# First stage of a transformer block: products begun on unnormalised tokens, norm factors put in behind the product

## The chip, the core and the metric

The kernel runs on one core of a Trainium2 chip. The core has TensorE (PE: matmuls; PEld is its weight load), VectorE (DVE), ScalarE (ACT), GpSimd (POOL) and SyncE (SP, which here only issues DMAs). Each engine works through its own queue of instructions in order; a matmul writes a bank of PSUM, from where VectorE or ScalarE read it. The metric is the device time of one execution in microseconds; lower is better. Three runs of the kernel before gave 1831.18, 1831.6 and 1834.9 us.

## The reference

One layer in fp32 for 1024 tokens of width 1024: a half-weighted SwiGLU feed-forward (inner width 2816), a mixer (short convolution and gated delta rule), another half-weighted feed-forward, and a last norm. The change touches the first feed-forward's input side alone:

```python
def rmsnorm(x, w, eps=NORM_EPS):
    xf = x.astype(jnp.float32)
    y = xf * lax.rsqrt(jnp.mean(xf * xf, axis=-1, keepdims=True) + eps)
    return (y * w.astype(jnp.float32)).astype(x.dtype)

def swiglu_ffn(x, w_in, w_out):
    gate, up = jnp.split(x @ w_in, 2, axis=-1)
    return (jax.nn.silu(gate) * up) @ w_out

h = h + 0.5 * swiglu_ffn(rmsnorm(h, ffn1_norm[layer]), ffn1_w_in[layer], ffn1_w_out[layer])
```

The norm's factor is one number per token, the gain one number per column of x. So the factor of a token can be put in on either side of the product with `w_in`.

## The kernel before

**Numbers.** Each fp32 operand is split into a rounded high part and the rest (`split`, L104 on ScalarE for the high part, L105 on VectorE for the low part), and a product is three matmuls: hi by hi (L197), lo by hi (L198), hi by lo (L199), function `mm3`. Tiles are 128 x 512; x lies transposed, so that a column of a tile is a token and a row one of 1024 inputs: 8 tiles for the first 512 tokens (`h[0]`), 8 for the others (`h[1]`).

**Pairs.** The gate and up weights are worked through in 22 pairs of 128 columns. A pair is a 2 x 2 block product by a Strassen-like scheme with seven products instead of eight, each of 4 quarters of the sum times 3 matmuls = 12 matmuls. In words of the code: the *first product* (A11 x B11, `run_p1`), whose bank is copied to SBUF (`copy_p1`, L387, ScalarE); the *second product* (A12 x B21, `run_p2`), summed onto the first in the same bank, which gives block C11, read by ScalarE's silu (L510); the two products of sums S1 x T1 and nS2 x T2; p7 (S3 x T3), p4 (A22 x T4) and p3 (S4 x B22). The first and second products are a pair's *heads*: they need only the first tokens, no sums. S1, S2, S3, S4 are sums of token tiles (`Blocks.sums`, L331/L332 and what follows), T1 to T4 sums of weight tiles (L112 on POOL, for the first two pairs L117 on VectorE), and all are split before use.

**Order.** Tasks with a load, a preparation and a run are issued in a written order; the loads go ahead on SP's queue, the preparations some tasks ahead of the runs, and sums, norm and stores hang on a count of the matmuls (`later`). A scheduler then orders what is not pinned (`keep_in_program_order`). In the first stage, the heads of five pairs (EARLY) come first, then the first two pairs' S1 T1 and nS2 T2 together, quarter by quarter (`both`), then the heads of the sixth pair; p7 of the first two pairs and the heads of the seventh follow (INSIDE = 2). From the third pair on, a pair's heads lie inside the pair ahead of it.

**The start.** The eight tiles of the first tokens are loaded first; ScalarE squares each (L240), VectorE adds the squares up (L242), four matmuls by ones give the column sums (L248), VectorE and POOL make the factor (L223, L225), and four transposes spread it over the partitions into a PSUM bank (L271). Meanwhile TensorE does 34 + 6 + 5 matmuls of zeros (L708), whose result nobody reads. Then each tile is multiplied by gain and factor (`norm1`, L307) and split, and the first product of four pairs is done quarter by quarter. The factor of the other 512 tokens comes from token rows (`xtok`; `row_square`, `by_rows`), is spread by L271 too, and goes in with the sums; `begin2` (L317, L318) prepares those tiles.

## Time and profile before

| what | us |
|---|---|
| median of three runs | 1831.6 |
| the profiled execution's own time | 1828.37 |
| its span | 1826.6 |
| TensorE busy | 1791.3 |
| VectorE, ScalarE, POOL busy | 1309.4, 737.2, 680.6 |

The page adds up one execution: busy time and count of each engine, the span in slices, the chain that ended last, and groups of instructions. A matmul's row in a timeline gives start and length; matmuls overlap, so the distance between starts is what one costs. The mean granted TensorE clock over the span was 0.994 of full speed.

### The profile page before, as it was taken

To read this page: it belongs to the slowest core of one execution; us is meant where nothing else is said; L and a number is where in the kernel's file an instruction comes from. 1 tells how busy PE (TensorE), PEld (TensorE's weight loads), DVE (VectorE), ACT (ScalarE), POOL (GpSimd) and SP (SyncE) were. 2 spreads that over 40 slices of the span, in tenths; PEclk is the share of its full clock that TensorE was granted. 3 is DMA by queue.
4 is the path that set the end of the run, shared out by engine and by line. 5 is a ranking of instruction groups with operands and counts; after the bars stand their busy time and mean duration, and the time that the engine had idled before them with its cause. 6 is when DMAs were issued, how large, how long until landed. Compare 5 with 4: busy or idle time off the path is not lost.

```text
span 1826.6 us, 24897 instructions
## 1 busy us (share of the span) xinstructions
PE 1791.3 (98%) x8508; PEld 1463.7 (80%) x8509; DVE 1309.4 (72%) x2040; ACT 737.2 (40%) x1478; POOL 680.6 (37%) x478
## 2 busy tenths in 40 slices
PE   9999999999999999999989999999999999999997
PEld 6788888888888887777778887788888888888886
DVE  8966666567766888977857566888656666677675
ACT  7423232323534554476342343552223222254443
POOL 0365554446342402234421113006544554435252
PEclk9999999999999999999989999999999999999998
DMA  7253443337974543488754485523443343488642
GB/s 260 70 172 116 146 137 126 134 116 226 317 265 144 170 141 123 131 253 268 232 160 147 133 277 179 188 76 115 151 144 115 137 146 126 170 292 281 203 142 89
DMA packets 194320, 311.41 MB, mean 170 GB/s; under 512 B 28176, under 2 KB 48656, under 8 KB 194192
## 3 DMA queue, kind: packets, MB, share of 16 engines
q1 hardware_dynamic: 191168, 304.51, 50.1%
q10 hardware_dynamic: 3024, 5.30, 0.9%
q8 instruction: 67, 1.10, 0.2%
q14 instruction: 61, 0.50, 0.1%
HBM read 226.87 MB, written 82.86 MB: 170 GB/s over the span
## 4 chain that ended last, share of the span: by engine, by line
PE 85%; DVE 6%; DMA 3%; issue 2%; ACT 2%; POOL 1%; SPq 0%; ACTq 0%; POOLq 0%; DVEq 0%
PE ps_ps L197 24%; PE ps_ps L199 24%; PE ps_ps L198 24%; PE ps_mm L197 3%; PE ps_mm L198 2%; PE ps_mm L199 2%; DVE cv L884 1%; PE ps_aux L982 1%; DVE wlo L105 1%; DVE sv L1135 1%; DVE xb L1139 1%; DMA raw<-w_in 1%; DMA h<-xT 1%; PE ps_aux L1008 0%; PE ps_ps L799 0%
## 5 line engine op out<-in xcount | busy, mean ns | idle before, releaser
L197 PE MATMUL ps_ps<-hi,whi 128*128 128x512 f32 x1400 | 545.8, 391 | 3.7 <-DVE h L1469 1.5
L198 PE MATMUL ps_ps<-lo,whi 128*128 128x512 f32 x1400 | 545.1, 389 | 0.1
L199 PE MATMUL ps_ps<-hi,wlo 128*128 128x512 f32 x1400 | 544.7, 390 | 0.1
L105 DVE TENSOR_TENSOR wlo<-T,whi 128x512 fp32r<-128x512 f32 x244 | 225.8, 939 | 131.6 <-ACT whi L104 130.9
L112 POOL TENSOR_TENSOR T<-raw 128x512 f32<-128x512 f32 x132 | 206.9, 1568 | 299.7 <-DVE wlo L105 112.8
L197 PEld LDWEIGHTS ps_ps<-hi,whi 128*128 128x128 f32 x1400 | 262.7, 188 | 63.4 <-ACT p L387 2.6
L105 DVE TENSOR_TENSOR wlo<-raw,whi 128x512 fp32r<-128x512 f32 x280 | 247.2, 893 | 90.5 <-ACT whi L104 86.9
L199 PEld LDWEIGHTS ps_ps<-hi,wlo 128*128 128x128 f32 x1400 | 262.8, 188 | 56.2 <-DVE wlo L105 1.5
L198 PEld LDWEIGHTS ps_ps<-lo,whi 128*128 128x128 f32 x1400 | 262.9, 188 | 54.7 <-DVE lo L105 0.8
L197 PE MATMUL ps_ps<-ghi,whi 128*128 128x512 f32 x616 | 241.3, 392 | 0.0
L199 PE MATMUL ps_ps<-ghi,wlo 128*128 128x512 f32 x616 | 240.9, 391 | 0.4 <-DVE wlo L105 0.4
L198 PE MATMUL ps_ps<-glo,whi 128*128 128x512 f32 x616 | 240.6, 391 | 0.0
L104 ACT CAST whi<-raw 128x512 fp32r<-128x512 f32 x280 | 169.1, 618 | 58.5 <-DMA raw<-w_in 21.8
L104 ACT CAST whi<-T 128x512 fp32r<-128x512 f32 x244 | 146.3, 616 | 75.7 <-POOL T L112 34.3
L105 DVE TENSOR_TENSOR glo<-raw,ghi 128x512 fp32r<-128x512 f32 x154 | 129.0, 838 | 51.4 <-ACT ghi L104 51.3
L197 PE MATMUL ps_mm<-hi,whi 128*128 128x512 f32 x384 | 158.0, 411 | 1.2 <-DVE u L452 1.2
L198 PE MATMUL ps_mm<-lo,whi 128*128 128x512 f32 x384 | 151.9, 396 | 0.0
L199 PE MATMUL ps_mm<-hi,wlo 128*128 128x512 f32 x384 | 151.6, 395 | 0.0
L199 PEld LDWEIGHTS ps_ps<-ghi,wlo 128*128 128x128 f32 x616 | 115.8, 188 | 26.5 <-DVE wlo L105 1.0
L198 PEld LDWEIGHTS ps_ps<-glo,whi 128*128 128x128 f32 x616 | 116.1, 188 | 25.6
L197 PEld LDWEIGHTS ps_ps<-ghi,whi 128*128 128x128 f32 x616 | 115.7, 188 | 25.2
L387 ACT COPY p<-ps_ps 128x512 f32<-128x512 f32 x50 | 29.0, 585 | 240.4 <-PE ps_ps L199 239.4
(238 smaller groups left out, 2259.8 us busy)
## 6 DMA issues: line engine op xcount, KB each, us to landing
raw<-w_in SPq DMA_DIRECT2D x264, 256.0 KB, 4.5
raw<-w_out SPq DMA_DIRECT2D x154, 256.0 KB, 4.4
raw<-w_qkv SPq DMA_DIRECT2D x36, 256.0 KB, 3.1
f1S<-S SPq DMA_DIRECT2D x33, 256.0 KB, 4.9
raw<-f1A SPq DMA_DIRECT2D x33, 256.0 KB, 4.1
raw<-f1S SPq DMA_DIRECT2D x33, 256.0 KB, 3.7
f2S<-S SPq DMA_DIRECT2D x33, 256.0 KB, 4.9
raw<-f2A SPq DMA_DIRECT2D x33, 256.0 KB, 4.5
```

Source lines behind the costliest of these rows:

```text
L104: tc.keep_in_program_order(nc.scalar.copy(out=hi, in_=src))
L105: nc.vector.tensor_tensor(out=lo, in0=src, in1=hi.bitcast(F32), op=ALU.subtract)
L112: tc.keep_in_program_order(nc.gpsimd.tensor_tensor(out=out, in0=in0, in1=in1, op=op))
L197: nc.tensor.matmul(out=ps, lhsT=whi, rhs=xhi, start=start, stop=False, skip_group_check=True)
L198: nc.tensor.matmul(out=ps, lhsT=whi, rhs=xlo, start=False, stop=False, skip_group_check=True)
L199: nc.tensor.matmul(out=ps, lhsT=wlo, rhs=xhi, start=False, stop=stop, skip_group_check=True)
L387: ins = nc.scalar.copy(out=self.p1[:, 3:HALF + 3], in_=self.x_ps)
L884: nc.vector.scalar_tensor_tensor(out=acc, in0=u[:, i:i + HALF], scalar=vcol(wc + i), in1=acc, op0=ALU.mult, op1=ALU.add)
L982: nc.tensor.matmul(out=ps[:, sl], lhsT=lhs[:, sl], rhs=rhs[:, sl], start=start, stop=stop)
L1135: nc.vector.tensor_tensor(out=tv, in0=lrow[:, lo:hi].unsqueeze(2).broadcast_to([nb, n, j + 1]), in1=xrow[:, 0:j + 1].unsqueeze(1).broadcas ...
L1139: nc.vector.tensor_tensor(out=xv, in0=xv, in1=tv, op=ALU.subtract)
```

## The change

The first tokens are split as they land, with their gain but without the norm's factor. The first product of four pairs begins on them while the squares are still being summed. The column sums stand ahead of the last quarter of those products, the spread of the factor behind it. ScalarE copies the factor from PSUM to SBUF (`rb0`, which shares a buffer with a tile of a later stage), and it goes in when a bank is read: the first product's bank is read by VectorE with a multiply (new L388) in place of ScalarE's copy, and C11 by VectorE with a multiply (new L510), which is followed by the silu on ScalarE in SBUF (new L512). This holds for all 22 pairs. The tiles themselves are multiplied by the factor later, for the sums S2, S3 and S4. The squares of token rows, that multiply and `begin2` are spread over the tasks of the heads. There are 12 matmuls of zeros instead of 45. The first four weight tiles are loaded between the first and the second token tile, the token rows later. The heads of six pairs stand ahead of the sums instead of five, and of one pair instead of two inside.

```diff
+        def landed(self, d):
+            sq = slot(F32, "sq")
+            tc.keep_in_program_order(nc.scalar.activation(out=sq, in_=self.hh[d], func=AF.Square))
+            if d:
+                nc.vector.tensor_tensor(out=self.acc, in0=self.acc, in1=sq, op=ALU.add)
+            else:
+                self.acc = sq
...
         def copy_p1(self):
             self.p1 = temp4(F32, "p1")
-            ins = nc.scalar.copy(out=self.p1[:, 3:HALF + 3], in_=self.x_ps)
-            if self.pinned:
-                tc.keep_in_program_order(ins)
+            if self.rb is None:
+                nc.scalar.copy(out=self.p1[:, 3:HALF + 3], in_=self.x_ps)
+            else:
+                nc.vector.tensor_tensor(out=self.p1[:, 3:HALF + 3], in0=self.x_ps, in1=self.rb, op=ALU.mult)
...
         def first(ps):
             c = temp4(F32, "c11")
+            if rb is not None:
+                nc.vector.tensor_tensor(out=c[:, 3:HALF + 3], in0=ps, in1=rb, op=ALU.mult)
+                ps = c[:, 3:HALF + 3]
             nc.scalar.activation(out=c[:, 3:HALF + 3], in_=ps, func=AF.Silu)
...
+        def split_raw(d):
+            src, gain = h[0][d], x.gain(d)
+            hi, lo = slot(F32R, "hi"), slot(F32R, "lo")
+            tc.keep_in_program_order(nc.scalar.activation(out=hi, in_=src, func=AF.Copy, scale=gain))
+            nc.vector.scalar_tensor_tensor(out=lo, in0=src, scalar=gain, in1=hi.bitcast(F32),
+                                           op0=ALU.mult, op1=ALU.subtract)
+            x.b["A11" if d < KH else "A12"][d % KH] = hi, lo
...
-            get_x(0, *range(KT))
-            tc.keep_in_program_order(nc.sync.dma_start(out=cs, in_=cst))
+            get_x(0, 0)
             for p in four:
                 p.get("B11")
+            get_x(0, *range(1, KT))
+            tc.keep_in_program_order(nc.sync.dma_start(out=cs, in_=cst))
...
-            norms[0].as_they_land(idle)
-            norms[0].spread()
-            idle(5)
+            for _ in range(12):
+                tc.keep_in_program_order(
+                    nc.tensor.matmul(out=idle_ps, lhsT=zero[:, 0:P], rhs=zero, start=True, stop=True))
             for p in four:
                 p.x_ps = psum()
-                p.ready("B11")
+            for k in range(KH):
+                split_raw(k)
+                if k == 0:
+                    for p in four:
+                        p.ready("B11")
+                norms[0].landed(k)
+            for d in range(KH, KT):
+                norms[0].landed(d)
+            for d in range(KH, KT):
+                split_raw(d)
...
+            def scaled():
+                norms[0].spread()
+                nc.scalar.copy(out=rb0, in_=norms[0].rb)
+                for p in four:
+                    p.w.pop("B11")
+                    p.copy_p1()
...
+            more = {1: (lambda: squares(0, 1), None),
+                    2: (lambda: squares(2, 3, 4), lambda: get_rows(0, 1)),
+                    3: (lambda: (squares(5, 6, 7), norms[1].by_rows()), lambda: get_rows(2, 3)),
+                    4: (lambda: norm1(0, 1, 2, 3), lambda: get_x(1, 0, 4, 1, 5, 2, 6, 3, 7)),
+                    5: (lambda: [x.begin2(k) for k in range(KH)], None)}
...
-            for k in range(1, KH):
+            for k in range(KH - 1):
                 task(lambda k=k: run(k))
+            task(norms[0].all_landed)
+            task(lambda: run(KH - 1))
+            task(scaled)
             task(*early[4].head1())
-            for p in early:
-                task(*p.head2())
-
-        g_dr = ffn_in(x, norms, w1_in, "f1", first_heads)
+            for i in range(4):
+                second(i, early[i])
+            task(norms[1].spread)
+            second(4, early[4])
+            task(*early[5].head1())
+            second(5, early[5])
+            task(None, lambda: norm1(4, 5, 6, 7))
+
+        g_dr = ffn_in(x, norms, w1_in, "f1", first_heads, rb0, 6, 1)
```

On TensorE at the start of the program, before (one "zero" row for each length of matmuls of zeros; out is left of the arrow):

```order
L708 MATMUL ps_ps<-zero 128x512
L248 MATMUL ps_ps<-one,sq 128x1 x4
...
L271 MATMUL ps_ps<-cs,rs 128x128 x4
...
L197 MATMUL ps_ps<-hi,whi 128x512 x4
L198 MATMUL ps_ps<-lo,whi 128x512
L199 MATMUL ps_ps<-hi,wlo 128x512
```

The same place in the changed kernel:

```order
L709 MATMUL ps_ps<-zero 128x512
L197 MATMUL ps_ps<-hi,whi 128x512
L198 MATMUL ps_ps<-lo,whi 128x512
L199 MATMUL ps_ps<-hi,wlo 128x512
...
L247 MATMUL ps_ps<-one,sq 128x1 x4
L197 MATMUL ps_ps<-hi,whi 128x512
...
L269 MATMUL ps_ps<-cs,rs 128x128 x4
```

The column sums (L248, now L247) and the spread (L271, now L269) stood ahead of all products; now 36 matmuls of products stand ahead of the sums and 12 more ahead of the spread.

On VectorE where the operands of the sums are made, before. Numbers tell tiles apart: h_75 to h_78 and h_83 to h_86 are token tiles, ps_ps_534 the second tokens' factor, raw and T1, T2 weight tiles and their sums.

```order
L331 TENSOR_TENSOR h_84<-h_84,ps_ps_534 128x512
L105 TENSOR_TENSOR lo_573<-h_75,hi_572 128x512
L105 TENSOR_TENSOR wlo_579<-raw_448,whi_578 128x512
L332 TENSOR_TENSOR h_76<-h_76,h_84 128x512
L105 TENSOR_TENSOR lo_597<-h_84,hi_596 128x512
L117 TENSOR_TENSOR T1_606<-raw_468,raw_466 128x512
L331 TENSOR_TENSOR h_85<-h_85,ps_ps_534 128x512
```

The same place in the changed kernel, from the read of the fourth pair's C11 (ps_ps_225) on; ps_ps_598 is the second tokens' factor, ps_ps_650 the sixth pair's bank:

```order
L510 TENSOR_TENSOR c11_591<-ps_ps_225,rb0_74 128x512
L105 TENSOR_TENSOR wlo_549<-raw_426,whi_548 128x512
...
L510 TENSOR_TENSOR c11_643<-ps_ps_483,rb0_74 128x512
L316 SCALAR_TENSOR_TENSOR h_83<-h_87,vs_66,h_83 128x512
...
L329 TENSOR_TENSOR h_84<-h_84,ps_ps_598 128x512
L105 TENSOR_TENSOR wlo_618<-T2_615,whi_617 128x512
...
L329 TENSOR_TENSOR h_85<-h_85,ps_ps_598 128x512
L388 TENSOR_TENSOR p1_673<-ps_ps_650,rb0_74 128x512
```

Reads of PSUM banks (L510, L388), `begin2` (L316) and weights of the sixth pair now stand in VectorE's queue between the operands of the sums; from the read of C11 to the read of the sixth pair's first product there are 20 rows between. The next read of a first product (the seventh pair's) stands 36 rows further.

On TensorE around the second products of the sixth and seventh pair, before (ps_ps_816 is the sixth pair's bank, ps_ps_707 the bank of the first pair's p7):

```order
L199 MATMUL ps_ps_715<-hi_632,wlo_661 128x512
L197 MATMUL ps_ps_816<-hi_328,whi_702 128x512
...
L199 MATMUL ps_ps_816<-hi_347,wlo_703 128x512
L197 MATMUL ps_ps_707<-hi_746,whi_790 128x512
...
L198 MATMUL ps_ps_707<-lo_755,whi_790 128x512
L197 MATMUL ps_ps_816<-hi_405,whi_724 128x512
```

And in the changed kernel (ps_ps_650 the sixth pair's bank, ps_ps_834 the seventh's, ps_ps_722 and 723 the first pair's sums, of which the second takes up p7):

```order
L199 MATMUL ps_ps_650<-hi_262,wlo_549 128x512
L197 MATMUL ps_ps_722<-hi_605,whi_646 128x512
...
L199 MATMUL ps_ps_723<-hi_639,wlo_618 128x512
L197 MATMUL ps_ps_650<-hi_281,whi_567 128x512
...
L199 MATMUL ps_ps_834<-hi_262,wlo_719 128x512
L197 MATMUL ps_ps_723<-hi_760,whi_802 128x512
...
L198 MATMUL ps_ps_723<-lo_769,whi_802 128x512
L197 MATMUL ps_ps_834<-hi_281,whi_740 128x512
```

The sixth pair's first product moved from behind `both` to ahead of it; its second product stands behind 12 matmuls of `both`. The seventh pair took the sixth's old place: behind its first product come five matmuls of p7 and then its second product.

87 lines of the change are left out of this document (32 added, 55 removed).

## The prediction, as put on record before the changed kernel was timed

> **What bounds the kernel now.** I read the page first, then busy time by stretch, then TensorE's waits in the first stage.
>
> ```profile
> span 1826.6 us, 24897 instructions
> PE 1791.3 (98%) x8508; PEld 1463.7 (80%) x8509; DVE 1309.4 (72%) x2040; ACT 737.2 (40%) x1478; POOL 680.6 (37%) x478
> ```
> TensorE is busy for 98% of the span: an edit pays only where TensorE waits or does work that is not needed. The next view gives stretches: start and end, length, busy time (and instructions) of PE, PEld, DVE, ACT, POOL, then granted clock, DMA share and GB/s.
>
> ```profile
> 0.00:17.57 17.57, 13.98 (x57) 6.14 (x58) 9.24 (x18) 9.48 (x17) 3.09 (x9) 1.00 0.93 333
> 15.00:20.00 5.00, 4.04 (x18) 2.52 (x19) 3.99 (x8) 3.10 (x8) 0.37 (x1) 1.00 1.06 406
> 17.57:48.03 30.46, 30.29 (x133) 24.19 (x133) 30.43 (x53) 27.21 (x57) 1.46 (x1) 1.00 0.55 199
> 48.03:71.00 22.97, 22.97 (x101) 18.61 (x100) 21.70 (x35) 10.04 (x18) 2.91 (x2) 1.00 0.32 103
> 71.00:120.00 49.00, 48.32 (x213) 39.71 (x213) 40.38 (x51) 17.08 (x30) 32.80 (x21) 1.00 0.32 108
> 240.00:280.00 40.00, 40.00 (x178) 33.14 (x177) 25.18 (x30) 10.87 (x20) 18.57 (x12) 1.00 0.44 141
> ```
> The first 17.57 us hold no product, only idle matmuls and the norm; that is what the change goes for. From there to 71 us TensorE stands still for hardly 0.2 us, and **VectorE is all but full too**: 30.43 of 30.46, then 21.70 of 22.97. It has slack only later, 25 of 40 us. So where TensorE starts earlier, VectorE must have its operands earlier. TensorE's waits to 460 us (total, times, longest):
>
> ```profile
> PE ps_ps L248 <- DVE sq L242: 1.4, 1, 1.4
> PE ps_ps L197 <- ACT p L387: 0.7, 1, 0.7
> PE ps_ps L197 <- ACT hi L104: 0.4, 1, 0.4
> ```
>
> **The lead that the change makes.** TensorE and its weight loads at the start, then the landings:
>
> ```profile
> 1.31 9.94 PE L708 MATMUL ps_ps<-zero 128*128 128x512 bf16 x34 [1.31 <-DVE zero L702]
> 1.72 0.15 PEld L708 LDWEIGHTS <-zero 128*128 128x128 bf16 x1 [0.27 <-issue]
> 2.14 0.15 PEld L708 LDWEIGHTS <-zero 128*128 128x128 bf16 x1 [0.28 <-issue]
> 12.64 1.05 PE L248 MATMUL ps_ps<-one,sq 128*128 128x1 f32 x8 [1.39 <-DVE sq L242]
> 13.56 1.46 PE L708 MATMUL ps_ps<-zero 128*128 128x512 bf16 x6
> 17.57 1.19 PE L197 MATMUL ps_ps<-hi,whi 128*128 128x512 f32 x4 [0.41 <-ACT hi L104]
> 28.98 0.60 PE L271 MATMUL ps_ps<-cs,rs 128*128 128x128 f32 x4
> 29.34 0.48 PE L197 MATMUL ps_ps<-hi,whi 128*128 128x512 f32 x1
> ```
> ```profile
> L685 SPq DMA_DIRECT2D h<-xT x16: 327/358/432, 0.8 to 17.8; - x16
> DMA to landing us min/median/max: 3.0/5.1/5.2
> ```
> And what one operation costs on VectorE, ScalarE and POOL:
>
> ```profile
> 7.18 3.08 DVE L242 TENSOR_TENSOR sq<-sq 128x512 f32<-128x512 f32 x4 [0.39 <-ACT sq L240]
> 24.07 2.49 DVE L105 TENSOR_TENSOR lo<-h,hi 128x512 fp32r<-128x512 f32 x4
> 26.74 2.74 DVE L318 SCALAR_TENSOR_TENSOR h<-h,vs 128x512 f32<-128x512 f32 x4
> 59.71 0.69 DVE L105 TENSOR_TENSOR wlo<-T,whi 128x512 fp32r<-128x512 f32 x1
> 77.75 0.69 DVE L447 TENSOR_TENSOR p<-ps_ps,p 128x512 f32<-128x512 f32 x1 [0.28 <-PE ps_ps L199]
> 28.45 2.17 ACT L104 CAST whi<-raw 128x512 fp32r<-128x512 f32 x4
> 30.52 2.01 ACT L387 COPY p<-ps_ps 128x512 f32<-128x512 f32 x4
> 13.97 1.40 POOL L225 TENSOR_TENSOR rs<-ms,cs 128x4 f32<-128x4 f32 x1 [11.69 <-DVE ms L223]
> ```
> A matmul starts every 0.227 us (22.97 / 101), so a product of 12 (four quarters by three matmuls) takes 2.72. On VectorE a tensor operation starts every 0.60 us ((2.49 - 0.69) / 3) and lasts 0.69; one with a scalar every 0.68 ((2.74 - 0.69) / 3), chained adds up to 0.80 ((3.08 - 0.69) / 3). ScalarE starts a cast every 0.52 ((30.52 - 28.45) / 4).
>
> Idle matmuls start 0.42 us apart there (2.14 - 1.72): twelve end at 1.31 + 5.1 = 6.4. By then h0 (0.8 + 3.0 = 3.8) and four weight tiles (one per 0.65 us: 256 KB at 406 GB/s; the last at 6.4) are there or one cast from use, so the **first product starts near 6.4 instead of 17.57**. Three quarters of four products take 8.2 us, and h1 comes behind the four weights, about 0.6 late: 15.2. The column sums want the eighth square added. From the second lo (9.7) VectorE has ten rows to do, adds and lo mixed, at 0.60 to 0.80: 16.3, TensorE loses 1.2. Sums 0.92 (13.56 - 12.64), last quarter 2.72, transposes 0.36 (29.34 - 28.98): the fifth pair starts at **20.4 instead of 29.34, a lead of 8.9**. The mean and POOL's power (1.40) are hidden by the last quarter's 2.72; without it they would cost 1.6. The loads that moved on SP's queue come in time: the second weights of the four pairs are its tiles 14 to 17, there by 3.8 + 17 x 0.65 = 14.9 and used from 23; the sixth pair's are the 36th and 37th, there by 27.9 and used at 35. Its rows and second-half tiles between them are covered by the same margin.
>
> **Where the lead goes.** All products wait for VectorE's queue, which has more in it now. From the factor on, each first product is read by VectorE where ScalarE copied it, and each C11 by VectorE ahead of ScalarE's silu.
>
> *First stall.* TensorE goes through five second products and the sixth pair's first product in 20.4 + 7 x 2.72 + 0.4 (the rows' factor's transposes, now in here) = 39.9. VectorE reads the fourth pair's sum when TensorE ends it (34.25, five products after 20.4 and the drain of 0.28 as in the 77.75 row). That is a wait which VectorE did not have there: queued behind it are the sixth pair's weights, the begin2 rows and all operands of "both", for which TensorE waits next. The weights stand on ScalarE behind the silu of that sum and a cast: 36.2. From there: two wlo, one sum, four begin2 (3 x 0.60 + 4 x 0.68 = 4.5), and the read of the sixth pair's first product stands 13 rows further (7.8): it starts at 48.5 and ends at 49.2. Its second product waits for that, and of "both" only 12 matmuls stand ahead of it (2.7). **9.3 - 2.7 = 6.6 lost.** So the sixth pair is not wholly ahead of the sums.
>
> *Second stall.* The seventh pair's first product is read 36 VectorE rows after the sixth's: 32 x 0.60 + 4 x 0.68 = 21.9, so it starts at 70.4 and ends at 71.1. TensorE from 49.2 has its second product (2.72), 36 of "both" (8.2), the seventh's first (2.72) and five matmuls of p7 (1.1), 14.7 in all. **21.9 - 14.7 = 7.2 lost**; before, this read stood in ScalarE's queue.
>
> Then p4 of the second pair writes a bank that VectorE, 1 us behind TensorE there, reads late: 0 to 0.9; I take 0.9, since nothing between lets VectorE catch up. From the fifth pair's start to the end of the first pair's p4 lie 204 matmuls, 46.3 us. Before: 77.75 - 29.34 = 48.4, so 2.1 with its own waits and drain. After: 20.4 + 46.3 + 0.4 + 6.6 + 7.2 + 0.3 = 81.2. That is **+3.4, and +4.3 with the 0.9**.
>
> **Not shown before, so bounded.** The two gaps hold 5.1 us (39.9 to 45.0: T2 ends as VectorE's fifth row behind 40.7, at 43.8, and ScalarE casts T2 and then T1, 1.2) and 4.8 us (63.9 to 68.7: the last S3 tile ends as the 31st row behind 48.5, 67.5, and ScalarE casts it and then T3, 1.2) with no matmul at all. The one such gap of this trace lies at 923 to 927 us (columns as above):
>
> ```profile
> PE ps_aux L1008 <- DMA xc<-diag_x: 4.6, 1, 4.6
> 926.00:928.00 2.00, 0.61 (x17) 0.60 (x17) 0.33 (x2) 0.69 (x3) 0.00 (x0) 0.97 0.42 66
> 928.00:930.00 2.00, 2.00 (x18) 1.25 (x20) 0.88 (x3) 1.91 (x7) 0.00 (x0) 0.50 0.21 33
> 932.00:935.00 3.00, 3.00 (x13) 2.15 (x12) 0.74 (x2) 1.21 (x5) 0.20 (x1) 0.55 0.29 87
> 935.00:938.00 3.00, 3.00 (x30) 2.93 (x31) 2.39 (x6) 1.98 (x11) 1.84 (x2) 1.00 0.00 0
> ```
> After 4.6 us without work the granted clock was 0.50 for about 6.8 us (928 to 934.7). The same here would cost at most 1.5 behind the first gap (seven matmuls and part of a product at half speed, less 0.5 of slack of the row that reads it) and 2.2 behind the second (71.1 to 75.5 at half speed): 0 to 3.7. One case of one says "yes", the phase is unknown: I take 1.7.
>
> The Trainium skill, "TensorE: Matmul & The Clock Gate", What's actually happening, says that a free-running window of about 3.4 us without activity halves the clock, and a busy one gives it back. The trace agrees on the halving (4.6 us, then 0.50) and shows it to last two such windows. By that rule gaps of 5.1 and 4.8 us hold a whole window in 4 to 5 of 10 phases; this term would be near 1.6 by the rule, 3.7 if every gap did as the one seen.
>
> New VectorE rows could be stretched while POOL works:
>
> ```profile
> L432 DVE TENSOR_TENSOR u<-ps_ps,p 128x512 f32<-128x512 f32 x20 | 13.6, 678 | 0.0
> L521 DVE TENSOR_TENSOR u<-u,c 128x512 f32<-128x512 f32 x22 | 27.4, 1247 | 0.1
> L387 ACT COPY p<-ps_ps 128x512 f32<-128x512 f32 x22 | 12.6, 584 | 113.6 <-PE ps_ps L199 113.6
> ```
> Operations from PSUM and one buffer keep 678 ns, those from two buffers go to 1247. The new evictions are of the first kind: 0.69. Other rows at 70 to 78 us may be stretched by POOL's next sums: 0 to 2, I take 0.5. In the steady state VectorE gets 2 x 0.60 = 1.2 to 1.4 us per pair of 19 us (7 products): 25 of 40 becomes 28 of 40, hidden by p7's 12 matmuls (2.72) between the read of a first product and its second one. Nothing; with that cover gone up to 0.7 a pair, some 10 over 15 pairs. ScalarE loses 22 copies (12.6 us) and waits less; worth nothing, it is idle half the time.
>
> Sum: 4.3 + 1.7 + 0.5 = **+6.5**: 1828.4 of the profiled execution becomes 1834.9. The runs' median is 3.2 above that execution, so I put it on the median: 1831.6 + 6.5 = 1838.1.
>
> **Rivals.**
> *The lead survives* (faster). Without either stall the sum is 20.4 + 46.3 + 0.4 + 0.3 = 67.4, -10.4: 1821; with half of them 1828. For it: 11 us of idle start do go, and before, VectorE kept up at 95%. Against: it decides only if the 49 rows from 40.7 to 70.4 take 25 us, at 0.50 a row; the trace has 0.60.
> *Just eaten* (within 0.2%, 3.7 us, about what a measurement here can tell from no change): full clock and 3 us less of stall, as when the sixth pair's casts come ahead of the silu (1.2, and its like later): +1.5, 1833.
> *Clock lost behind both gaps*, and POOL at its bound: 4.3 + 3.7 + 2 = +10, 1841.6.
> *VectorE bounds the pairs*: 4.3 + 10, 1846. Against: 12 idle us of 40.
>
> **How the numbers follow.** Forecast 0.51 (own range 1835.5 to 1840.5); lead survives 0.10; just eaten 0.15; clock lost 0.20; VectorE bound 0.04. Slower 0.75, same 0.15, faster 0.10. The range 1832.5 to 1843.5 leaves out the faster cases and the last rival.
>
> **What would show it.** First product near 6.4, fifth pair near 20.4 (right for the lead). Waits of TensorE on the VectorE line that evicts first products near 49 and 71 us, with VectorE full from 21 to 71; clock below 1 near 45 or 69; no new waits after 90 us. If the pair's line shows no such waits, or VectorE has idle time before 49, the prediction is wrong.

## The result: slower by 10.9 us, and the profile after

| | before | changed |
|---|---|---|
| median of six runs each, us | 1831.51 | 1842.42 |
| lowest to highest, us | 1830.15 to 1835.12 | 1839.29 to 1846.0 |
| the profiled execution, us | 1828.37 | 1844.62 |
| its span, us | 1826.6 | 1842.9 |

The ratio of the changed kernel's runs to those of before is 1.0058, with a 95% interval of 1.0047 to 1.0068. The forecast was 1838.1 and slower. The side holds and the time lies inside the range, but outside the likeliest case's own range (1835.5 to 1840.5); the last sections say which term was too small.

From the page of the changed kernel, busy time and count of each engine:

```profile
PE 1794.3 (97%) x8476; PEld 1465.3 (80%) x8476; DVE 1341.9 (73%) x2084; ACT 729.5 (40%) x1457; POOL 683.9 (37%) x478
```

TensorE has nearly the same busy time in a longer span: what is new is waiting. Its two largest groups of waits in the first 460 us (total, times, longest) name the places:

```profile
PE ps_ps L197 <- ACT whi L104: 5.3, 2, 5.0
PE ps_ps L197 <- DVE u L413: 4.4, 1, 4.4
```

Three waits were in the prediction with a place and a size: 5.1 (found 5.0), 4.8 (4.4) and 0.9 (0.9, the row of 85.18 below). The timeline of TensorE shows them in order (start, length, then in brackets the idle time ahead and what ended it):

```profile
6.05 0.99 PE L197 MATMUL ps_ps<-hi,whi 128*128 128x512 f32 x1
16.83 1.05 PE L247 MATMUL ps_ps<-one,sq 128*128 128x1 f32 x8 [1.28 <-DVE sq L239]
20.95 0.48 PE L197 MATMUL ps_ps<-hi,whi 128*128 128x512 f32 x1
45.70 0.79 PE L197 MATMUL ps_ps<-hi,whi 128*128 128x512 f32 x1 [4.96 <-ACT whi L104]
70.21 0.80 PE L197 MATMUL ps_ps<-hi,whi 128*128 128x512 f32 x1 [4.43 <-DVE u L413]
85.18 0.50 PE L197 MATMUL ps_ps<-hi,whi 128*128 128x512 f32 x1 [0.89 <-DVE c L440]
160.56 0.47 PE L197 MATMUL ps_ps<-hi,whi 128*128 128x512 f32 x1 [0.80 <-DVE p L388]
```

Products begin at 6.05 instead of 17.57 and the fifth pair at 20.95 instead of 29.34. That lead of 8.4 us is gone before the second gap begins. To compare the two orders at any moment, I count product matmuls (L197 to L199) and take the start of the same-numbered one in both traces. Both kernels have 7200 of them. The 308th starts at 90.02 before and at 97.78 in the changed kernel, a shift of +7.8 us; I call this the shift at 90 us. It runs so, by the time of before:

| time before, us | 26 | 43 | 49 | 57 to 60 | 68 | 80 to 127 | 165 | 203 | 450 |
|---|---|---|---|---|---|---|---|---|---|
| shift, us | -8.5 | -8.4 | -3.4 | +0.2 | +7.3 | +7.8 | +9.3 | +9.6 | +11.75 |

So the first gap and the half clock behind it eat the lead, the second gap puts the kernel 7.8 us behind, and a slow creep adds 4.0 until the last pair: 0.5 by 139 us, 1.05 at 151 us, and from there 0.35 per two pairs. After that nothing of the change is left to act. The first store of tokens behind the feed-forward marks its end in both kernels (the rows give shortest, median and longest issue in ns, then first and last start in us). First before, then changed:

```profile
L771 SPq DMA_DIRECT2D h_dr<-h x8: 319/320/326, 624.4 to 655.6; - x8
```

```profile
L797 SPq DMA_DIRECT2D h_dr<-h x8: 319/320/327, 636.1 to 667.3; - x8
```

At the store the shift is 11.7 us; the two spans differ by 16.3. The last 4.6 arise in the mixer, where neither kernel differs. The profiled execution of before was the fastest shown (1828.37, 3.1 below its median), that of the changed kernel 2.2 above its own, so I count those 4.6 as the spread of single executions: the medians differ by 10.9, close to the 11.7.

Granted clock and load of each engine in the stretches that matter (length, then busy time and count of PE, PEld, DVE, ACT, POOL, then clock, DMA share, GB/s):

```profile
21.00:45.00 24.00, 19.74 (x90) 16.00 (x88) 21.68 (x37) 16.54 (x35) 1.45 (x1) 0.99 0.55 205
45.00:50.00 5.00, 4.30 (x10) 3.05 (x11) 5.00 (x9) 2.49 (x5) 0.00 (x0) 0.50 0.00 0
...
71.00:75.00 4.00, 3.99 (x10) 2.75 (x9) 3.99 (x7) 1.24 (x2) 1.13 (x1) 0.50 0.33 104
38.00:72.00 34.00, 24.23 (x88) 17.96 (x87) 33.18 (x56) 13.93 (x24) 0.00 (x0) 0.85 0.17 54
```

Both gaps are followed by a clock of 0.50, and from 38 to 72 us VectorE works 33.18 of 34 us while TensorE is busy for 24. The first 71 us as a whole, before and then changed:

```profile
0.00:71.00 71.00, 67.25 (x288) 48.94 (x289) 61.37 (x104) 46.73 (x90) 7.45 (x12) 1.00 0.57 201
```

```profile
0.00:71.00 71.00, 58.41 (x234) 43.84 (x234) 61.64 (x105) 41.30 (x78) 4.70 (x10) 0.93 0.51 186
```

VectorE has 104 instructions and 61.4 us in the one, 105 and 61.6 in the other: as many rows in the same time. They are not the same rows: 12 of the 105 are the new reads (six L388, six L510), and about as many of the rows that before has done by then are still to come. TensorE started 11.5 us earlier, VectorE got nothing done sooner.

### The profile page after: what moved, and what is told of

Its sections match the earlier page's. It is cut to its first block, busy times and chain, and to the rows that moved or that the text cites. A ratio compares the mean times of both kernels' runs of the same rounds, so it can differ in the third digit from the quotient of the medians.

```text
span 1842.9 us, 24942 instructions
## 1 busy us (share of the span) xinstructions
PE 1794.3 (97%) x8476; PEld 1465.3 (80%) x8476; DVE 1341.9 (73%) x2084; ACT 729.5 (40%) x1457; POOL 683.9 (37%) x478
## 4 chain that ended last, share of the span: by engine, by line
PE 84%; DVE 8%; DMA 2%; issue 2%; ACT 2%; POOL 1%; SPq 0%; ACTq 0%; POOLq 0%; DVEq 0%
PE ps_ps L197 24%; PE ps_ps L199 24%; PE ps_ps L198 24%; PE ps_mm L197 3%; PE ps_mm L199 2%; PE ps_mm L198 2%; DVE wlo L105 1%; PE ps_aux L1008 1%; DVE cv L910 1%; DVE sv L1161 1%; DVE xb L1165 1%; DVE lo L105 1%; PE ps_aux L1034 1%; DMA raw<-w_in 0%; PE ps_aux L1014 0%
## 5 line engine op out<-in xcount | busy, mean ns | idle before, releaser
L197 PE MATMUL ps_ps<-hi,whi 128*128 128x512 f32 x1400 | 550.1, 394 | 14.8 <-ACT whi L104 5.3
L198 PE MATMUL ps_ps<-lo,whi 128*128 128x512 f32 x1400 | 547.3, 391 | 0.3 <-DVE lo L693 0.2
L199 PE MATMUL ps_ps<-hi,wlo 128*128 128x512 f32 x1400 | 546.5, 391 | 0.0
L197 PEld LDWEIGHTS ps_ps<-hi,whi 128*128 128x128 f32 x1400 | 264.2, 189 | 79.1 <-ACT whi L104 12.9
L199 PEld LDWEIGHTS ps_ps<-hi,wlo 128*128 128x128 f32 x1400 | 263.8, 188 | 57.0 <-DVE wlo L105 1.8
L198 PEld LDWEIGHTS ps_ps<-lo,whi 128*128 128x128 f32 x1400 | 264.2, 189 | 55.0 <-DVE lo L105 0.8
L105 DVE TENSOR_TENSOR wlo<-T,whi 128x512 fp32r<-128x512 f32 x244 | 229.8, 951 | 90.2 <-ACT whi L104 87.9
L197 PE MATMUL ps_ps<-ghi,whi 128*128 128x512 f32 x616 | 241.3, 392 | 0.0
L199 PE MATMUL ps_ps<-ghi,wlo 128*128 128x512 f32 x616 | 240.9, 391 | 0.4 <-DVE wlo L105 0.4
L198 PE MATMUL ps_ps<-glo,whi 128*128 128x512 f32 x616 | 240.5, 390 | 0.0
L197 PE MATMUL ps_mm<-hi,whi 128*128 128x512 f32 x384 | 158.2, 412 | 1.2 <-DVE u L451 1.2
L198 PE MATMUL ps_mm<-lo,whi 128*128 128x512 f32 x384 | 151.8, 395 | 0.0
L199 PE MATMUL ps_mm<-hi,wlo 128*128 128x512 f32 x384 | 151.6, 395 | 0.0
L199 PEld LDWEIGHTS ps_ps<-ghi,wlo 128*128 128x128 f32 x616 | 115.8, 188 | 26.6 <-DVE wlo L105 1.1
L198 PEld LDWEIGHTS ps_ps<-glo,whi 128*128 128x128 f32 x616 | 116.0, 188 | 25.5
L197 PEld LDWEIGHTS ps_ps<-ghi,whi 128*128 128x128 f32 x616 | 115.7, 188 | 25.2
L104 ACT CAST ghi<-raw 128x512 fp32r<-128x512 f32 x154 | 95.0, 617 | 70.4 <-DMA raw<-f2A 19.1
```

Source lines behind the costliest of these rows:

```text
L104: tc.keep_in_program_order(nc.scalar.copy(out=hi, in_=src))
L105: nc.vector.tensor_tensor(out=lo, in0=src, in1=hi.bitcast(F32), op=ALU.subtract)
L197: nc.tensor.matmul(out=ps, lhsT=whi, rhs=xhi, start=start, stop=False, skip_group_check=True)
L198: nc.tensor.matmul(out=ps, lhsT=whi, rhs=xlo, start=False, stop=False, skip_group_check=True)
L199: nc.tensor.matmul(out=ps, lhsT=wlo, rhs=xhi, start=False, stop=stop, skip_group_check=True)
```

## Experiments

The theory on test was the prediction's: the new reads (L388, L510) in VectorE's queue delay the operands of the sums, so TensorE stalls twice, and each stall costs some clock on top. Rivals were that the clock is most of it, that the sixth pair ahead of the sums is at fault, and, once the creep was seen, that later pairs are slowed by something else than the reads. The table gives the shift at 90 us and at the store (each against the trace of before), and medians against runs of before on the same chip. A short name is used in the text.

| run | what it changes | at 90 us | at the store | median, us | ratio (95%) |
|---|---|---|---|---|---|
| changed kernel | | +7.8 | +11.7 | 1842.42 | 1.0058 (1.0047 to 1.0068) |
| e1_fill | zeros in both gaps | +6.4 | +10.1 | 1841.12 | 1.0054 (1.0036 to 1.0071) |
| e2_five_two | five pairs ahead, two inside | +7.7 | +12.3 | 1840.4 | 1.0048 (1.0033 to 1.0063) |
| e3_plain | no factor at the reads, all pairs | +6.3 | +6.5 | 1840.0 | 1.0047 (1.0032 to 1.0063) |
| e4_late_plain | the same for pairs 8 to 22 | +9.3 | +10.4 | 1840.57 | 1.0045 (1.003 to 1.006) |
| e5_order | begin2 earlier, S4 later | +7.1 | +11.1 | 1843.75 | 1.0064 (1.0048 to 1.008) |
| e6_evict_alone | before, with the reads alone | +11.9 | +15.8 | 1844.54 | 1.0064 (1.0047 to 1.008) |
| e7_plain_order | e3 and e5 together | +1.5 | +2.7 | 1836.35 | 1.003 (1.0018 to 1.0042) |
| e8_order_fill | e5 with zeros in the gaps | +8.1 | +12.3 | 1845.69 | 1.0071 (1.0056 to 1.0086) |
| e9_begin2_fill | begin2 earlier, zeros | +6.7 | +10.5 | 1839.25 | 1.0046 (1.0031 to 1.0061) |
| e10_plain_begin2 | e3, begin2 earlier | +1.4 | +2.5 | 1835.61 | 1.0027 (1.0016 to 1.0039) |

The medians of before beside them were 1832.2 (e1 to e4), 1831.23 (e5 to e8) and 1831.91 (e9, e10).

### Is it the clock? (e1_fill)

Matmuls of zeros into a bank that is rewritten afterwards keep TensorE at work in the gaps:

```diff
-            task(*early[5].head1())
+            f, g, l = early[5].head1()
+            task(lambda: (f(), idle_into(early[4].x_ps, 20)), g, l)
...
-                task(*p.head1())
+                f, g, l = p.head1()
+                task((lambda: (f(), idle_into(pairs[5].x_ps, 18))) if n_early == 6 else f, g, l)
```

> The changed kernel with 20 matmuls of zeros behind the sixth pair's first product and 18 behind the seventh's, where TensorE stood still for 5.0 and 4.4 us and the granted clock fell to 0.50 behind. Nothing else moves. At 90 us the changed kernel is 7.8 us behind the kernel before, at the first store of tokens (624 us in the kernel before) 11.7. Theory (the stalls come from VectorE's queue, the clock is an extra): clock 1.00 from 40 to 80 us, VectorE still full, TensorE's real products still wait for the same reads; the second product of the sixth pair starts 1.3 us earlier (it started 1.4 after its bank was read), the seventh pair's second product and half-speed matmuls give another 1.0 to 1.3: 5.3 to 5.8 behind at 90 us, 9.3 to 9.8 at the store, time near 1840. Rival (the clock is most of the loss): 3 or less behind at 90 us, time under 1837.

The same two stretches as above, in e1:

```profile
45.00:50.00 5.00, 3.72 (x14) 2.20 (x13) 5.00 (x9) 2.47 (x5) 0.00 (x0) 1.00 0.00 0
71.00:75.00 4.00, 4.00 (x20) 3.27 (x19) 3.14 (x7) 1.24 (x2) 2.05 (x1) 1.00 0.42 131
```

The clock stays at 1.00 and the shift at 90 us falls from 7.8 to 6.4, at the store from 11.7 to 10.1. The clock's share is thus 1.4 us, or 1.6 at the store (the last 0.2 arose behind 90 us, where the clock is 1.00 in both kernels); the run's shift lies 0.6 above what was expected. The rival that the clock is most of it falls. Some of it had been passed on by VectorE: in the changed kernel VectorE waits 0.82 us for a sum that TensorE made partly at half speed, in the row of 54.23 (the other two are the reads of the sixth and seventh pair's first products):

```profile
49.13 0.68 DVE L388 TENSOR_TENSOR p<-ps_ps,rb 128x512 f32<-128x512 f32 x1
...
54.23 0.69 DVE L510 TENSOR_TENSOR c<-ps_ps,rb 128x512 f32<-128x512 f32 x1 [0.82 <-PE ps_ps L199]
...
71.91 0.68 DVE L388 TENSOR_TENSOR p<-ps_ps,rb 128x512 f32<-128x512 f32 x1
```

With the zeros, p7 of the first pair starts at 69.29 instead of 70.21, 0.9 earlier. From there on TensorE, at full clock, has to wait for VectorE's rows, 1.5 us in these two groups of waits (e1, 55 to 90 us), which half clock had hidden:

```profile
PE ps_ps L198 <- DVE lo L105: 1.0, 2, 0.7
PE ps_ps L199 <- DVE wlo L105: 0.5, 1, 0.5
```

### Is it the sixth pair? (e2_five_two)

```diff
-            task(*early[5].head1())
-            second(5, early[5])
+            task(None, lambda: [x.begin2(k) for k in range(KH)])
...
-        g_dr = ffn_in(x, norms, w1_in, "f1", first_heads, rb0, 6, 1)
+        g_dr = ffn_in(x, norms, w1_in, "f1", first_heads, rb0, 5, 2)
```

> The changed kernel with the heads of five pairs ahead of the sums and two inside, as before the change; begin2 gets a task of its own. Theory (VectorE's queue): the same rows stand in VectorE's queue, so the products of the sums wait as much, only at other places: TensorE's gaps 3.7 and 2.5 us in place of 5.0 and 4.4, later second products 0.9 us later; with a clock that falls once or not at all 6.0 to 8.5 behind the kernel before at 90 us (7.8 in the changed kernel), time 1840 to 1843. Rival (the sixth pair ahead of the sums is at fault): 4 or less behind at 90 us, time 1838 or less.

The shift at 90 us is the same (+7.7), with three waits instead of two:

```profile
PE ps_ps L197 <- ACT whi L104: 9.6, 3, 5.3
```

The shift lies where it was expected, the waits do not: the last gap is 5.3 us instead of 2.5, and the clock fell twice (40.15 and 64.04 us). Fewer products ahead of the sums only move the same waiting. The "one pair more" of the change is neither the fault nor a help.

### Is it the reads? (e3_plain, e4_late_plain)

e3 gives no factor to any pair, so ScalarE copies the first product and the silu reads PSUM, as before; e4 leaves the factor out from the eighth pair on. Everything else stands.

```diff
-        pairs = [gate_pair(x, w_in, j, gs, store, rb) for j in range(NJ)]
+        pairs = [gate_pair(x, w_in, j, gs, store, None) for j in range(NJ)]
```

(in e4: `rb if j < 7 else None`)

> The early start alone: the changed kernel, but the first products are copied by ScalarE and C11 goes straight to the silu for all 22 pairs, as before the change; the norm's factor is left out of both, so this part of the computation is missing, with the work on VectorE for it. Theory (VectorE's queue): 12 rows (7.2 us) less ahead of p7, all but two reads of banks off VectorE: 0.5 to 2 us behind the kernel before at 90 us (7.8 in the changed kernel), no further loss to the first store of tokens, time 1831 to 1834: the lead of 8.5 us is eaten even so, since the sums' rows fill VectorE from 21 to 70 us. Rival (the reads on VectorE are the whole fault): the lead is kept, 8 us ahead at 90 us, time 1823. Rival (order on TensorE or the loads): 4 or more behind.

> The changed kernel, with the factor's multiplies on VectorE for the first seven pairs alone; pairs 8 to 22 have ScalarE's copy and the silu from PSUM as before the change, and their factor is left out of C11 and the first product. To 90 us the same as the changed kernel, 7.8 behind. Theory (the first product's read stands behind a stretched split of weights in VectorE's queue, 0.25 to 1.0 us per pair or two): no further loss, 7.6 to 8.2 behind at the first store of tokens in place of 11.7, time near 1838.5. Rival (the later steps come from elsewhere): 11 to 12 behind there, time 1842.

e3 was a miss, and the one that mattered: without a single new read, +6.3 at 90 us, where I had expected at most 2. VectorE was not full there; it stood still. Its timeline, ScalarE's, and the wait of TensorE that follows:

```profile
37.87 1.29 DVE L105 TENSOR_TENSOR wlo<-raw,whi 128x512 fp32r<-128x512 f32 x2 [3.66 <-ACT whi L104]
41.73 0.68 DVE L329 TENSOR_TENSOR h<-h,ps_ps 128x512 f32<-128x512 f32 x1
...
36.73 0.60 ACT L512 ACTIVATE c<-ps_ps 128x512 f32<-128x512 f32 x1 [2.12 <-PE ps_ps L199]
37.23 1.13 ACT L104 CAST whi<-raw 128x512 fp32r<-128x512 f32 x2
38.26 2.57 ACT L315 ACTIVATE h<-h,vs 128x512 f32<-128x512 f32 x4
...
68.88 1.28 PE L197 MATMUL ps_ps<-hi,whi 128*128 128x512 f32 x2 [5.40 <-DVE u L413]
```

It reads as one chain of queues: the silu of the fourth pair (36.73) waits 2.12 us for TensorE's second product; the sixth pair's weight casts (37.23) and begin2's ScalarE half (38.26) stand behind it on ScalarE; VectorE's wlo rows wait for those casts (3.66), begin2 stands behind the wlo rows, and the first row of the sums (L329) comes at 41.73. Between 31 and 38 us VectorE worked 0.82 of 7 us:

```profile
31.00:38.00 7.00, 7.00 (x35) 5.80 (x34) 0.82 (x3) 4.82 (x9) 1.02 (x1) 1.00 0.21 76
```

In the changed kernel that row comes at 41.31, in before at 31.80 (both rows stand in the section on p7 below). So the sums begin 9.5 us **later**, although TensorE began 11.5 us earlier, and the reads are not what decides it.

What the reads do cost is the creep. From 90 us to the store the shift grows by 0.25 us in e3, 1.1 in e4 and 4.0 in the changed kernel. In the changed kernel 3.5 of the 4.0 lie in eight steps, each right ahead of a second product: 1.05 at 160.56 us, then 0.35 at every second pair until 429.66. e3 and e4 have none of these steps, so they are the work of the reads of pairs 8 to 22. What e4 loses is something else, and it had been expected to lose nothing: it comes at 141 to 149 us, 60 us and more behind its last read (78.45), where a row of VectorE that TensorE needs (L441, at 148.10) stands behind the low part of a weight whose cast waits until 146.84 for its load. e10 below has the same 1.1 without any read; why it differs from e3 is open. The rows behind the first step, at 160 us of the changed kernel (VectorE, then POOL):

```profile
156.34 3.47 DVE L105 TENSOR_TENSOR wlo<-T,whi 128x512 fp32r<-128x512 f32 x2
159.74 0.68 DVE L388 TENSOR_TENSOR p<-ps_ps,rb 128x512 f32<-128x512 f32 x1
...
157.52 1.75 POOL L112 TENSOR_TENSOR S<-u,nS 128x512 f32<-128x512 f32 x1
159.23 1.72 POOL L112 TENSOR_TENSOR T<-raw 128x512 f32<-128x512 f32 x1
```

Two wlo rows (both operands in SBUF) take 1.7 us each while POOL adds, instead of 0.68; the read itself (one operand in PSUM) keeps 0.68 although POOL adds then too (159.23), but it stands behind them, and TensorE's second product (160.56 above) waits 0.80 for it. Before, ScalarE made this copy and had no such rows ahead of it. The Trainium skill, "SBUF — State Buffer", Who interferes with whom, states that a VectorE operation with two SBUF inputs contends with GpSimd's reads and one with at most one SBUF input does not. The trace agrees with both halves (1.7 against 0.68 us).

e4's +9.3 at 90 us is above the changed kernel's +7.8 for another reason, which the section on what was unexpected gives.

### The reads without the early start (e6_evict_alone)

The kernel before, with both reads on VectorE (a multiply by a tile of ones):

```diff
+    rb0 = const.tile([P, HALF], F32, name="rb0", tag="rb", bufs=1)
+    nc.gpsimd.memset(rb0, 1.0)
...
-        g_dr = ffn_in(x, norms, w1_in, "f1", first_heads)
+        g_dr = ffn_in(x, norms, w1_in, "f1", first_heads, rb0)
```

(and the lines of `copy_p1`, `gate_pair` and `first` as in the change)

> The reads alone: the kernel before with its start, its five pairs and its factor as they were, but each first product and each C11 read by VectorE with a multiply by a tile of ones, in place of ScalarE's copy and silu from PSUM. Theory (VectorE has no room between 17.6 and 71 us): ten to twelve rows more (6.0 to 7.2 us) come straight onto TensorE's time, with the waits that a read in VectorE's queue brings: 6 to 10 behind the kernel before at 90 us, and 3 to 4.5 more in the later pairs, 10 to 14 at the store, time 1841 to 1846. Rival (the reads are hidden, the loss is that of the early start): under 2 at 90 us, time 1834 or less.

+11.9 at 90 us, more than expected; its time of 1844.54 is what was expected. Its trace is of its longest execution, 9.5 above its median, so only the first 90 us are used. Some 5 us are a wait that before did not have:

```profile
27.49 1.98 DVE L392 TENSOR_TENSOR p<-ps_ps,rb 128x512 f32<-128x512 f32 x3 [3.07 <-PE ps_ps L199]
32.39 0.15 DVE L263 TENSOR_TENSOR both<-tot 128x4 f32<-128x4 f32 x1
...
34.33 1.11 PE L271 MATMUL ps_ps<-cs,rs 128*128 128x128 f32 x4 [4.92 <-POOL rs L225]
```

The read waits 3.07 us for the first products, and the row that starts the second tokens' factor (L263) stands behind it; TensorE then waits 4.92 for that factor. Again it is one queue in order: a read of a product's bank stops all that stands behind it until TensorE gets there. As a whole this run does not price the reads, since it made a wait that the changed kernel does not have; the section on p7 uses the part of it that does.

### Can the order be mended? (e5_order, e8_order_fill, e7_plain_order)

If late begin2 rows delay the sums, they may go ahead of the sixth pair's weights. e5 puts them one task earlier, in the place of `norm1`, and moves the adds of S4 behind the splits of S3:

```diff
-                    4: (lambda: norm1(0, 1, 2, 3), lambda: get_x(1, 0, 4, 1, 5, 2, 6, 3, 7)),
-                    5: (lambda: [x.begin2(k) for k in range(KH)], None)}
+                    4: (lambda: [x.begin2(k) for k in range(KH)], lambda: get_x(1, 0, 4, 1, 5, 2, 6, 3, 7)),
+                    5: (lambda: norm1(0, 1, 2, 3), None)}
...
+                    s3 = temp(F32, "s3")
+                    nc.vector.tensor_tensor(out=s3, in0=s2, in1=a22, op=ALU.add)
+                    b["S3"][k] = split(s3, slot)
+            if part == 2:
+                for k in range(KH):
                     s4 = temp(F32, "s4")
                     self.s4.append(s4)
-                    nc.vector.tensor_tensor(out=s4, in0=h[0][k + KH], in1=s2, op=ALU.add)
-                    nc.vector.tensor_tensor(out=s2, in0=s2, in1=a22, op=ALU.add)
-                    b["S3"][k] = split(s2, slot)
-            if part == 2:
+                    nc.vector.tensor_tensor(out=s4, in0=h[0][k + KH], in1=h[0][k], op=ALU.add)
```

e8 adds zeros in the gaps (24 and 6 matmuls), e7 leaves the factor out as e3 does.

> The changed kernel with another order of the sums' preparation and nothing else: begin2 goes one task ahead of the factor's multiply of the first four token tiles (in the changed kernel it is behind), and S4's four adds go from ahead of S3's splits to behind them (in all three stages that use them). Theory (the lead is lost in the queues of VectorE and ScalarE, in what stands ahead of the sums' operands): the first sum's row starts at 38 instead of 41.3 us, and four rows (2.4 us) leave the way to p7: the shift at 90 us, with the clock still falling behind the first gap, 4.0 to 5.5 in place of 7.8; the later steps stay: 8 to 9.5 at the store, time 1838 to 1840. Rival (TensorE's order or the clock alone sets the loss): 7 to 8 at 90 us.

> The changed kernel with the other order of the sums' preparation, and matmuls of zeros in the two gaps (24 behind the sixth pair's first product, 6 behind the seventh's). Theory: clock 1.00 throughout, 2.2 to 4.0 behind the kernel before at 90 us, the later steps as in the changed kernel: 6 to 8 at the store, time 1836 to 1839. It would be the best form of this change with all its work in it, and still slower than the kernel before. Rival (order and clock together win the lead back): 0 or ahead at 90 us.

> The early start without the reads on VectorE (factor left out of the first products and C11 as in the early start alone) and with the other order of the sums' preparation. In the early start alone VectorE stood still for 6 us between 31 and 38, since ScalarE's casts and begin2 stood behind a silu that waited for TensorE. Theory (both the rows and their order eat the lead): with neither, part of the lead is there: 4 ahead to 0 at 90 us, no later steps, time 1827 to 1832. Rival (the early start brings nothing whatever VectorE does): 4 or more behind at 90 us, time 1837 or more.

All three miss on the slow side. e5's +7.1 is in its rival's 7 to 8, though not for the rival's reason: some 1.7 of it is a fall of the clock at the column sums (the last section has it), and the rest comes late. At 72 us e5's shift is only +0.6, e8's +0.3 and e7's -4.5: the mend works as far as p7. Then the adds that were moved are late. VectorE and TensorE of e5:

```profile
73.11 3.50 DVE L351 TENSOR_TENSOR s<-h 128x512 f32<-128x512 f32 x3
...
80.23 0.58 PE L197 MATMUL ps_ps<-hi,whi 128*128 128x512 f32 x1 [4.83 <-ACT hi L104]
```

Three of them take 3.50 us while POOL adds, and p3 waits 4.83 us for S4 (e8: 5.1, e7: 4.4). The stall moved from p7 to a later product; it did not get smaller.

### begin2 alone (e9_begin2_fill, e10_plain_begin2)

The first four lines of the diff above without the S4 part; e9 with the zeros of e8, e10 without the factor.

> The changed kernel with begin2 one task ahead of the factor's multiply (as in the other order), S4's adds where the changed kernel has them, and zeros in the two gaps (24 and 6). In the other order the four adds that went behind S3 came back at 73 to 80 us, stretched to 1.2 us each while POOL worked, and p4 waited 4.8 us. Theory (VectorE's queue): without that move the 2.3 us of the earlier begin2 stay: 3.5 to 5.0 behind the kernel before at 90 us (6.4 with zeros alone), 2 more if the clock falls at the column sums, then the later steps: 7 to 9 at the store, time 1837 to 1840. Rival (begin2's place is worth nothing): 6 to 7 at 90 us.

> The early start without the reads on VectorE (factor left out of first products and C11), with begin2 one task earlier and S4's adds where the changed kernel has them. Theory (rows and order on VectorE and ScalarE eat the lead): with the rows gone and begin2 no longer behind a silu, 3 ahead to 0 of the kernel before at 90 us, 2 less if the clock falls at the column sums; no later steps; time 1828 to 1832. It is the only one of these forms that is not slower than the kernel before. Rival (an early start cannot be kept, since the sums' rows alone fill VectorE to 88 us): 3 or more behind at 90 us, time 1835 or more.

e9's +6.7 lies inside what was expected once the 2 us named for a fall of the clock at the column sums are added, and that fall is in its trace; but its rival (6 to 7) covers the number too, so e9 decides nothing by itself. e10 against e3 does: begin2's place alone brings the first row of the sums from 41.73 to 35.33 and the shift from +6.3 to +1.4. As a forecast e10 missed, with 3 us ahead to 0 expected. It is the best form tried, and still slower than before, at a ratio of 1.0027 (1.0016 to 1.0039): no form of the early start beat the kernel before. Its first row of the sums, p7's start, and the stretches around them:

```profile
35.33 0.69 DVE L329 TENSOR_TENSOR h<-h,ps_ps 128x512 f32<-128x512 f32 x1 [0.95 <-PE ps_ps L269]
...
64.02 1.28 PE L197 MATMUL ps_ps<-hi,whi 128*128 128x512 f32 x2 [4.80 <-DVE u L413]
...
31.00:38.00 7.00, 7.00 (x34) 5.79 (x34) 5.38 (x9) 6.19 (x12) 0.00 (x0) 1.00 0.13 42
38.00:65.00 27.00, 20.65 (x87) 16.08 (x86) 27.00 (x45) 12.32 (x22) 0.00 (x0) 0.93 0.21 69
```

VectorE now works 5.38 of the 7 us in which it stood still in e3, and then 27.00 of 27 us. The lead is still 6.5 us at 63 us and is lost at once at p7, by a wait of 4.80 and the clock behind it.

### What sets the time up to p7

The p7 of the first pair is the first product on S3, and all rows of the sums up to S3 stand ahead of it on VectorE. What it waits for in the end is L413, the read of the bank that p7 goes on summing in, which stands behind the last of these rows; the cast of its weights (T3) ends on ScalarE at the same time, 70.15 us in the changed kernel. In before its start has no wait to mark it, but it can be told by its form: five matmuls of p7, the last an L198, then the second product's L197.

```profile
31.80 1.28 DVE L331 TENSOR_TENSOR h<-h,ps_ps 128x512 f32<-128x512 f32 x2
...
59.97 0.39 PE L197 MATMUL ps_ps<-hi,whi 128*128 128x512 f32 x1
...
61.03 0.40 PE L198 MATMUL ps_ps<-lo,whi 128*128 128x512 f32 x1
61.26 0.40 PE L197 MATMUL ps_ps<-hi,whi 128*128 128x512 f32 x1
```

The first row of the sums in the changed kernel, with begin2 ahead of it, and the last row ahead of p7:

```profile
38.66 2.73 DVE L316 SCALAR_TENSOR_TENSOR h<-h,vs 128x512 f32<-128x512 f32 x4
41.31 0.68 DVE L329 TENSOR_TENSOR h<-h,ps_ps 128x512 f32<-128x512 f32 x1
...
68.91 1.28 DVE L413 TENSOR_TENSOR u<-ps_ps,p 128x512 f32<-128x512 f32 x2
```

The kernels that keep S4's adds where they were, from the first row of the sums to p7's first matmul, with the VectorE rows that start in between:

| | first row of the sums | p7 starts | between | rows |
|---|---|---|---|---|
| before | 31.80 | 59.97 | 28.2 | 47 |
| changed kernel | 41.31 | 70.21 | 28.9 | 47 |
| e1_fill | 41.29 | 69.29 | 28.0 | 47 |
| e2_five_two | 37.77 | 64.63 | 26.9 | 45 |
| e3_plain | 41.73 | 68.88 | 27.2 | 45 |
| e4_late_plain | 43.15 | 71.85 | 28.7 | 47 |
| e9_begin2_fill | 40.11 | 68.80 | 28.7 | 48 |
| e10_plain_begin2 | 35.33 | 64.02 | 28.7 | 48 |
| e6_evict_alone | 37.72 | 69.41 | 31.7 | 53 |

In all but e6 that is 27 to 29 us, whether TensorE starts early or not: 45 to 48 rows at 0.60 us, with VectorE standing still for 0.8 us at most. e6 has six reads of banks in this stretch and takes 53 rows and 31.7 us, so a read that falls into it costs its 0.60 us; in the changed kernel only two do (49.13 and 54.23). From it the shifts follow. When p7 starts, the changed order has done 24 product matmuls more than before (204 instead of 180), 5.4 us at 0.227. So p7 comes 70.21 - 59.97 - 5.4 = 4.8 late in the changed kernel; the clock of 0.50 from there to 75.2 costs 2.5, the wait at p4 0.9, and the wait of 0.7 that before has at 71.89 is gone: +7.5 (measured +7.8). In e10 64.02 - 59.97 - 5.4 = -1.4, with 6 us at a clock of 0.66 behind the gap (2.0), p4's 1.4 and the 0.7: +1.3 (measured +1.4). In e3 68.88 - 59.97 - 5.4 = 3.5, with 4.1 us at 0.50 (2.1), 1.4 and the 0.7: +6.3 (measured +6.3). The start of the sums decides in all of them but e6, and each version has it later than before.

Why it was early before: the second tokens' factor was spread by TensorE at 28.98 and begin2's VectorE rows began at 26.74 with nothing in their queues that waited for products. In the changed kernel the spread starts at 34.67 and begin2 at 38.66. The row squares (L256) that the factor needs end on ScalarE at 29.7 instead of 26.1. They begin 4.3 us later (21.71 instead of 17.42), since the copy of the first tokens' factor (`rb0`, L737), which the change added, stands ahead of them and waits 3.15 us for TensorE; and the load of the silu's table and a silu stand ahead of the last one:

```profile
21.23 0.59 ACT L737 COPY rb<-ps_ps 128x512 f32<-128x512 f32 x1 [3.15 <-PE ps_ps L269]
21.71 0.64 ACT L256 ACTIVATE xtok<-xtok 128x512 f32<-128x512 f32 x1
...
27.18 1.28 ACT L512 ACT_TABLE_LOAD   x1
...
29.01 0.61 ACT L256 ACTIVATE xtok<-xtok 128x512 f32<-128x512 f32 x1
```

Whether a version with the second tokens' factor prepared first would bring the sums back to 31.8 and keep the lead was not tried. In e10 the sums wait 0.95 us for that very spread, and in both kernels TensorE comes to it (34.67 and 34.69) without a pause: so its place in TensorE's order would have to move as well.

## Why the prediction was right, and where it was not

**The lead.** First product 6.05 (predicted 6.4), wait ahead of the column sums 1.28 (1.2), fifth pair 20.95 (20.4): 8.4 instead of 8.9. Right.

**The first stall.** The gap was put at 39.9 to 45.0 and lies at 40.7 to 45.7; VectorE's read of the sixth pair's first product was put at 48.5 and stands at 49.13. Counting the rows in VectorE's queue and the 0.60 us of each was enough for that. Right, on the silu's row as well: "The weights stand on ScalarE behind the silu of that sum and a cast" is the chain that e3 shows.

**The second stall.** Read predicted at 70.4, found at 71.91, p7 at 68.7, found 70.21: 1.5 late. 0.6 of that is the start of the sums (41.31 instead of 40.7), 0.8 the wait of VectorE at 54.23 for a product made at half clock. The clock term was priced as lost on TensorE, with slack ahead of VectorE's reads; part of it came back through VectorE.

**The clock.** 1.7 was taken between 0 and 3.7; e1 measures 1.4 at 90 us and 1.6 at the store. Right. The clock fell inside both gaps, and it stayed low for some 5 us after work had begun again: 45.7 to 51.3 and 70.2 to 75.2.

**p4's bank.** 0.9 predicted and 0.89 found.

**The sum at 90 us** was 6.5 and came to 7.8. By e1 its terms are: the start of the sums 0.6 later; 1.5 of waits for VectorE's rows behind p7 where 0.5 had been taken (0 to 2 was the bound); the clock 1.4 instead of 1.7. That makes 6.5 + 0.6 + 1.0 - 0.3 = 7.8.

**The steady state is the step that failed.** The prediction says "hidden by p7's 12 matmuls (2.72) between the read of a first product and its second one. Nothing". Behind 90 us +4.0 came, 3.5 of it at such reads. The cover was counted against busy time (28 of 40 us), but what has to fit is the queue at one moment: wlo rows that POOL stretches to 1.7 us stand ahead of the read, and two of them use up the cover. The bound that was named for this, some 10 us over 15 pairs, was the right mechanism at a third of its size; in e4, which leaves those reads out, all 3.5 are gone. That the time still lies inside the range is luck in part: the room above 1838.1 was left for the clock and for POOL, and the later reads used it.

**The signs it named.** Two of its signs of being wrong are there. TensorE does not wait at the read of a first product near 49 and 71 us (the only such wait is at 160.56): the reads end at 49.81 and 72.59, while matmuls at half clock ahead of the second products last until 51.2 and 72.9. And VectorE was not full from 21 us on: it stands still for 2.3 of the 24 us to 45. The large waits lie at the operands of the sums, where the text had put them (39.9 to 45.0, 63.9 to 68.7); but the idle time belongs to the late start of the sums, which the next paragraph is about.

**The cause as told was half of it.** The prediction lays the stalls on VectorE, "which has more in it now". e3 and e10 show that the reads are not needed: without them the lead is lost too, with +6.3 and +1.4 at 90 us (some 1.7 of e3's is a fall of the clock that the changed kernel does not have; see the last section). The bound is VectorE's 27 to 29 us from the start of the sums, and the change delays that start by the order in ScalarE's and VectorE's queues. The rows that I counted were the right rows; that they would have been late without the new ones among them is what I had not asked.

**The rivals.** "The lead survives" falls with the waits; it would have needed rows of 0.50 us, and they were 0.60. "Just eaten" named 3 us less of stall and none of the clock; e1 has all of the clock and is not there. "Clock lost behind both gaps" gave 1841.6, near the time, but for the wrong reason: the clock cost 1.4 to 1.6, not 3.7. "VectorE bounds the pairs" is true to a third (3.5 of 10 us).

## What to carry to other kernels

Before an engine is started earlier, find the engine that feeds it and ask what it will have finished sooner: here VectorE was full from 18 us on in the kernel before. The time from the first row of the sums to p7 was 27 to 29 us in eight of nine versions (and longer in the one with six reads in it), so only an earlier start of that row, or fewer rows behind it, could win. An operation that reads a product's result, put into the queue of an engine which prepares operands, makes every operand behind it wait for the product; look at what stands behind it, not at the engine's busy share. For the steady state, compare the cover with the longest run of rows ahead of the read at that moment, in the durations that they have while another engine contends, and not with a mean.
